# A planner-ordered backbone kernel: the output products of a recurrence step are issued inside the next step, and the planner may hold TensorE for the chain

## The chip, the cores and the metric

One core of a Trainium2 chip runs the kernel. The metric is device time in microseconds (us), the median of several runs; lower is better. Engines are called by their names in the profile: PE is TensorE (PEld its weight loads), DVE is VectorE, ACT is ScalarE, POOL is GpSimd, SP is SyncE, which issues most DMAs.

## The reference, cut to what matters

Two layers, each: a modulated norm, one wide input projection, three token mixers side by side (convolution, attention, a recurrence in both directions over the tokens), a gated merge, an output projection and an MLP. The recurrence is what the change touches:

```python
def _rwkv_scan(r, w, k, v, kk, a, s0, reverse):
    def step(s, inp):
        r_t, w_t, k_t, v_t, kk_t, a_t = inp
        sa = jnp.einsum('bhij,bhj->bhi', s, -kk_t)
        s = (s * w_t[:, :, None, :] + sa[..., None] * (kk_t * a_t)[:, :, None, :]
             + v_t[..., None] * k_t[:, :, None, :])
        return s, jnp.einsum('bhij,bhj->bhi', s, r_t)
    s_fin, ys = lax.scan(step, s0, xs, reverse=reverse)
```

There are 8 heads of 64, 256 context and 512 latent tokens, and the two directions are added. The first layer needs the output `ys` of all tokens; the second layer only that of the latent tokens.

## The kernel before

**The recurrence in chunks.** Tokens are taken in chunks of 64, two heads (a pair) and both directions at once: 12 chunks for each of 4 pairs. A pair has two halves, a half has three pieces of two chunks. So a layer has 8 halves, 48 chunk steps. For each half `prepare` makes the decayed operands on DVE and ACT, `half_t` the masked products on PE (tile `tps`), `inverse` sends a triangular matrix through DRAM, inverts 16x16 blocks on DVE and loads the result `j` back by DMA, `half_solve` finishes the inverse on PE (tiles `wps`, `jps`, with `jt` made by DVE from `j`), and `token_major` transposes what the chain needs (`trps`, `vps`, `tvps`). Then `chain_piece` runs two chunk steps, each a row of hops between PE and the other engines:

- A: `ca<-x,ar`, the state X against this chunk's operand (PE), then `rhs` (DVE); meanwhile ACT makes the decayed state `xp`.
- B: `ca<-rhs,j` and `cb<-rhs,j`, the triangular solve (PE), then `gv` (one half on ACT, one on DVE).
- C: `ca<-gv,tok` (PE), then the next state X in two DVE additions.
- Y: the output products `psy<-tr,gv` and `psy<-ar,x` (PE), eight in a step, four in the first step of a pair. Nothing in the chain needs them. After a piece's second step ACT or DVE takes `psy` into `y`.

Before, the generator asks for PE for Y right after it has issued X, ahead of the next step's A.

**What sets the order.** The engines run in program order, and that order is written by a planner, `weave` (L282), when the program is built. Every stage is a set of generators (streams). A stream yields a time from which it can go on and the engine that it wants, and the planner keeps a clock for each engine (`spend`, L220, with a cost for each instruction). It always resumes the stream that could start first; on a near tie (EPS, 0.02 us) the one that stands first in the stage's order string. In the recurrence's stage (`phase_a`) the chain C stands first or, in the first layer, directly first ("CIEKAWLRGT"); G, the stream `products` of the big weight matrices (`mmps<-hh,wh` and its kin, with `wh`, `wl` and `hh`, `hl` the two parts of weights and activations), stands near the end and takes whatever time on PE the others leave. Products that the recurrence's stage doesn't place follow in the next stage, the attention (`attend`: `sps` scores, `ap` softmax, `atps` transposes into `aat`, then `mmps<-aat,avt`), and after it the merge.

Every matrix product of the kernel is issued by one line, L227 in `product` (L228 in the changed kernel, which has one more line above it), the transposes by L239, and DVE, ACT and POOL operations by L91, so rows are told apart by their tiles. One fp32 product shows as two MATMUL records in the trace, a main product (`mmps<-hh,wh`) as one.

Of the kernel before, what the change touches and what calls it, by code (L numbers as in the profile page):

```python
# [10 lines left out]
F32 = mybir.dt.float32  # L11
F32R = mybir.dt.float32r
I32 = mybir.dt.int32
AF = mybir.ActivationFunctionType
ALU = mybir.AluOpType
# [4 lines left out]
P = 128  # L20
# [31 lines left out]
SPARE = 1.5  # L52
EPS = 0.02
BLK = 1040
CTX = (0, NCTX)
# [64 lines left out]
class Trunk:  # L120
# [161 lines left out]
    def weave(self, order, streams, until=None):  # L282

        todo = self.todo
        todo += [[g, 0.0, "PE", None, None, k] for k, g in streams.items()]
        todo.sort(key=lambda s: order.find(s[5]) % 99)
        while todo and not (until and until()):
            best, at = None, 0.0  # L290
            for s in todo:
                held, names = self.held(s[4])
                if held is None or s[3] and not s[3]():
                    continue
                t = max(s[1], self.clock[s[2]], held)
                if best is None or t < at - EPS:
                    best, at, got, since = s, t, names, held
# [6 lines left out]
            try:  # L304
                y = next(best[0])
            except StopIteration:
                todo.remove(best)
                continue
            best[1:5] = y + (None, None)[len(y) - 2:]

    def running(self, keys):
        return any(s[5] in keys for s in self.todo)

# [881 lines left out]
    def half_solve(self, st):  # L1195
# [64 lines left out]
        self.x_t = max(self.x_t, t)  # L1260

    def chain_piece(self, pi, st, y, need_y):
        pr, S, V = self.pr, self.S, self.V
        hh, ar, pc = st["hh"], st["ar"], st["pc"]
        tr, tok, gv, j, tv = st["trs"][pi], st["toks"][pi], st["gvs"][pi], st["j"], st["tvs"][pi]
        gp = 3 * hh + pi
        self.x_t = max(self.x_t, st["tok_t"][pi])
        for q in range(2):
# [4 lines left out]
            yield self.x_t, "PE"  # L1273
            if need_y and q == 0:
                psy = self.rw.tile([P, 512], F32, tag="y", name="psy", bufs=1)[:, 0:256].rearrange("p (d c t) -> p d c t", d=2, c=2)
            ga = self.rw.tile([P, 512], F32, tag="ca", name="ca", bufs=1)
# [5 lines left out]
            else:  # L1282
                for d in range(2):
                    e = self.product(ga[gr[d], 0:128], ar[:, d, c, 0, :], X[:, d, :], start=True, stop=True,
                                     tile_position=(0, 64 * gd[d]))
                if not last:
                    xp = pr.tile([P, 2, 128], F32, tag="xp", name="xp", bufs=1)
                    for d in range(2):
                        S.activation(out=xp[:, d, :], in_=X[:, d, :], func=AF.Copy, scale=pc[:, d, c:c + 1])
                yield e, "DVE"  # L1290
                rhs = pr.tile([P, 128], F32, tag="rhs", name="rhs", bufs=1)
                t = V.tensor_tensor(out=rhs, in0=ga[:, 0:128], in1=tv[:, q, :], op=ALU.add)
                yield t, "PE"
            gps = [ga[:, 256:384], gb[:, 0:128]]
            for h in range(2):
                hc = slice(64 * h, 64 * h + 64)
                for d in range(2):
# [4 lines left out]
                    V.tensor_scalar(out=gv[gr[1], 2 + q, :], in0=gps[1][gr[1], :], scalar1=-1.0, scalar2=None, op0=ALU.mult))  # L1302
            yield t, "PE"
            if not last:
# [15 lines left out]
            if need_y:  # L1320
                yield t, "PE"
                for d in range(2):
                    for h in range(2):
                        hc = slice(64 * h, 64 * h + 64)
                        e = self.product(psy[hc, d, q, :], gv[:, 2 * d + q, hc], tr[:, q, gd[d], h, :],
                                         start=True, stop=first, tile_position=(0, 64 * h))
                        if not first:
                            e = self.product(psy[hc, d, q, :], X[:, d, hc], ar[:, d, c, 1, :],
                                             start=False, stop=True, tile_position=(0, 64 * h))
        if need_y:  # L1330
            yield e, "ACT" if gp in (0, 2, 3) else "DVE"
            t0 = [x - self.c0 for x in (128 * gp, 128 * (1 - gp) if gp < 2 else 896 - 128 * gp)]
            for d in range(2):
                src = psy[:, d].rearrange("p c t -> p (c t)")
                if d == 1:
                    src = src[:, ::-1]
                dst = y[:, t0[d]:t0[d] + 128]
                if gp in (0, 2, 3):
                    t = S.activation(out=dst, in_=src, func=AF.Copy)
                else:  # L1340
                    t = V.tensor_tensor(out=dst, in0=src, in1=dst, op=ALU.add)
            st["pp"]["y_t"] = t

# [102 lines left out]
    def chain(self, l, c0):  # L1446
        for n in range(8):
            p, hh = n // 2, n % 2
            pp = self.pairs[p]
            yield 0.0, "DVE", lambda: self.halves[n] is not None and "j_t" in self.halves[n]  # L1450
            st = self.halves[n]
            yield st["j_t"], "DVE"
            yield from self.half_solve(st)
            self.solved = n
            for pi in range(3):
# [4 lines left out]
                yield from self.chain_piece(pi, st, pp["y"], 128 * (3 * hh + pi) >= c0)  # L1460
                self.pieces[n] = pi
            if hh == 1:
# [33 lines left out]
    def inputs(self, l, full, lat):  # L1496
# [5 lines left out]
        self.ready, self.stage_t = {}, 0.0  # L1502
        self.conv_n, self.x_t = 0, 0.0
        self.n_upad = 2
        if len(lat) == 1:
# [705 lines left out]
```

## Time and profile before

| | |
|---|---|
| runs, us | 2950.61, 2959.81, 2959.90; median 2959.81 |
| profiled execution, us | 2955.57 (its span 2953.7) |
| mean granted TensorE clock | 0.98 |
| PE busy | 2802.2 us (95%) |
| DVE, ACT busy | 1964.8 us (67%), 1303.1 us (44%) |
| recurrence's stage | about 125 to 595 us (first layer), 1765 to 2262 us (second layer) |

Busy time is the union of an engine's instructions; PE's are pipelined and overlap. The view of stretches gives each engine's busy time between two moments; the timeline gives start and length of instructions in order, with the engine's idle time ahead of one in brackets and what ended it.

### The profile page before, as it was taken

The page shows a single profiled execution, that of the slowest core. Times are in us where ns is not written, and L with a number is a line of the kernel's source. Part 1 is how long each engine was busy: PE and PEld are TensorE (multiplying, and loading weights), DVE is VectorE, ACT ScalarE, POOL GpSimd, SP SyncE. Part 2 cuts the span into 40 slices and gives each one's busy share as a digit, 9 for nine tenths or more (in the row PEclk, how much of TensorE's full clock was granted, in tenths as well). Part 3 has the DMA queues.
Part 4 walks back from the last instruction along what each step waited for, and adds up shares of the span by engine and source line. Part 5 has one row for each costly group of instructions (what it writes and reads, how often), then busy time and mean ns, then how long its engine had stood idle before and what let it go on. Part 6 is the DMA issues. An engine that isn't in the chain of part 4 may idle for free.

```text
span 2953.7 us, 56336 instructions
## 1 busy us (share of the span) xinstructions
PE 2802.2 (95%) x22423; PEld 2236.2 (76%) x22423; DVE 1964.8 (67%) x4313; ACT 1303.1 (44%) x2522; POOL 106.7 (4%) x181
## 2 busy tenths in 40 slices
PE   8999999988999999999999999999999888899998
PEld 6777777777777887888888777776766656788887
DVE  6777777478996658764333569898894767644445
ACT  4556555455554224231313355555554564433333
POOL 0000001010000000000000000010000100000000
PEclk9999999999999999999999999999999999999999
DMA  5232233353227733553111222232334525422223
GB/s 207 64 80 74 60 86 93 92 160 113 85 75 271 265 125 115 175 188 110 63 65 67 96 72 84 74 84 70 82 109 145 162 89 161 139 93 97 94 96 104
DMA packets 247750, 330.96 MB, mean 112 GB/s; under 512 B 118256, under 2 KB 124032, under 8 KB 247360
## 3 DMA queue, kind: packets, MB, share of 16 engines
q1 hardware_dynamic: 242160, 311.63, 33.1%
q0 software_dynamic: 3712, 14.17, 1.9%
q8 instruction: 176, 2.88, 0.4%
q10 hardware_dynamic: 1616, 1.56, 0.2%
q14 instruction: 86, 0.70, 0.1%
HBM read 266.32 MB, written 47.60 MB: 106 GB/s over the span
## 4 chain that ended last, share of the span: by engine, by line
PE 75%; DVE 12%; ACT 4%; DMA 3%; issue 3%; SPq 0%; POOL 0%; DVEq 0%; ACTq 0%; POOLq 0%
PE mmps L227 60%; PE ca L227 3%; DVE cacc L91 2%; PE psy L227 2%; DVE wl L91 2%; PE tps L227 1%; ACT wh L91 1%; DVE ast L91 1%; PE sps L227 1%; PE tvps L227 1%; PE jps L227 1%; PE atps L239 1%; PE wps L227 1%; PE trps L239 1%; DVE jt L91 1%
## 5 line engine op out<-in xcount | busy, mean ns | idle before, releaser
L227 PE MATMUL mmps<-hh,wh 128*128 128x512 f32 (+1 forms) x2344 | 851.0, 363 | 21.9 <-DVE k L91 4.9
L227 PE MATMUL mmps<-hh,wl 128*128 128x512 f32 (+1 forms) x2344 | 848.2, 362 | 10.4 <-DVE wl L91 10.4
L227 PE MATMUL mmps<-hl,wh 128*128 128x512 f32 (+1 forms) x2344 | 847.7, 362 | 3.9 <-DVE hl L91 3.8
L91 DVE TENSOR_TENSOR wl<-wr,wh 128x512 fp32r<-128x512 f32 x596 | 412.3, 692 | 492.5 <-ACT wh L91 475.7
L91 ACT ACTIVATE wh<-wr 128x512 fp32r<-128x512 f32 x596 | 375.2, 630 | 741.2 <-PE mmps L227 681.7
L227 PEld LDWEIGHTS mmps<-hh,wh 128*128 128x128 f32 x2344 | 448.2, 191 | 92.1 <-issue 16.4
L227 PEld LDWEIGHTS mmps<-hh,wl 128*128 128x128 f32 x2344 | 447.7, 191 | 82.0 <-DVE wl L91 16.7
L227 PEld LDWEIGHTS mmps<-hl,wh 128*128 128x128 f32 x2344 | 448.5, 191 | 70.2 <-issue 7.2
L227 PE MATMUL mmps<-ffl,wh 128*128 128x512 f32 (+1 forms) x792 | 279.3, 353 | 0.0
L227 PE MATMUL mmps<-ffh,wh 128*128 128x512 f32 (+1 forms) x792 | 278.1, 351 | 0.0
L227 PE MATMUL mmps<-ffh,wl 128*128 128x512 f32 (+1 forms) x792 | 277.0, 350 | 0.0
L91 DVE SCALAR_TENSOR_TENSOR cacc<-upad,dww,cacc 128x783 f32<-128x783 f32 (+1 forms) x240 | 216.3, 901 | 4.4
L227 PEld LDWEIGHTS mmps<-ffh,wh 128*128 128x128 f32 x792 | 149.1, 188 | 22.7
L227 PEld LDWEIGHTS mmps<-ffh,wl 128*128 128x128 f32 x792 | 149.0, 188 | 21.5
L227 PEld LDWEIGHTS mmps<-ffl,wh 128*128 128x128 f32 x792 | 149.4, 189 | 20.7
L91 DVE SCALAR_TENSOR_TENSOR x<-mmps,mod,x 128x512 f32<-128x512 f32 (+1 forms) x126 | 80.1, 636 | 45.6 <-PE mmps L227 45.0
L91 POOL TENSOR_TENSOR bk<-bk,pc 128x384 f32<-128x384 f32 x64 | 59.3, 958 | 1230.0 <-PE tps L227 1230.0
L91 DVE SCALAR_TENSOR_TENSOR sq<-mmps,rl 128x512 f32<-128x512 f32 x96 | 56.9, 596 | 40.2 <-ACT rl L91 40.1
L91 ACT ACT_TABLE_LOAD x64 | 82.1, 1283 | 2.5 <-PE mmps L227 1.5
L91 DVE TENSOR_REDUCE ast<-sps 128x1 f32<-128x768 f32 (+1 forms) x80 | 67.5, 844 | 20.7 <-PE sps L227 20.7
L91 ACT ACTIVATE rl<-mmps 128x512 f32<-128x512 f32 x96 | 49.3, 515 | 67.9 <-PE mmps L227 67.9
L91 DVE TENSOR_TENSOR ffl<-sq,ffh 128x768 fp32r<-128x768 f32 (+1 forms) x64 | 52.7, 824 | 37.9 <-ACT ffh L91 37.7
(316 smaller groups left out, 4404.5 us busy)
## 6 DMA issues: line engine op xcount, KB each, us to landing
wr<-in_w_dram SPq DMA_DIRECT2D x268, 256.0 KB, 2.5
wr<-in_win_dram SPq DMA_DIRECT2D x236, 256.0 KB, 2.7
modw<-in_modw_dram SPq DMA_DIRECT2D x80, 512.0 KB, 4.5
wr<-in_pw_dram SPq DMA_DIRECT2D x48, 256.0 KB, 3.0
wr<-in_wo_dram SPq DMA_DIRECT2D x44, 256.0 KB, 2.6
g<-stage SPq DMA_DIRECT2D x24, 384.0 KB, 3.5
gate<-g SPq DMA_DIRECT2D x24, 384.0 KB, 3.7
scb<-in_modw_dram SPq DMA_DIRECT2D x16, 512.0 KB, 5.7
```

The source lines that it names most:

```text
L91: f(**kw)
L227: self.nc.tensor.matmul(out, lhsT, rhs, **kw)
L239: self.nc.tensor.transpose(out, src, self.ident)
```

## The change

The step's Y products are no longer issued by the step itself. The step leaves a job (`y_job`), and `y_products` issues it in the next step right behind A, before the generator yields for `rhs`. The evictions of `psy` (`y_outs`) come after that next step's `gv`. At a half's last piece the job is done at once. The mark `pieces`, by which other streams learn that a piece is through, is set in `y_outs`, so for the first two pieces of a half one step later than before.

And a stream may now yield a fifth value, a margin. With it the planner compares streams by max(ready, clock + margin, lock) - margin in place of max(ready, clock, lock): a stream that will be ready within STICK = 0.2 us of the engine's clock counts as ready now. The chain yields it ahead of B and ahead of C, not ahead of A.

```diff
+STICK = 0.2
@@ weave
-        todo += [[g, 0.0, "PE", None, None, k] for k, g in streams.items()]
+        todo += [[g, 0.0, "PE", None, None, 0.0, k] for k, g in streams.items()]
-                t = max(s[1], self.clock[s[2]], held)
+                t = max(s[1], self.clock[s[2]] + s[5], held) - s[5]
-            best[1:5] = y + (None, None)[len(y) - 2:]
+            best[1:6] = y + (None, None, 0.0)[len(y) - 2:]
@@
+    def y_products(self):
+        if self.y_job is None:
+            return
+        st, pi, q, X, first, y = self.y_job
+        self.y_job = None
...
+        if q == 0:
+            self.psy = self.rw.tile([P, 512], F32, tag="y", name="psy", bufs=1)[:, 0:256].rearrange("p (d c t) -> p d c t", d=2, c=2)
+        for d in range(2):
+            g = 1 - (q ^ d)
+            for h in range(2):
+                hc = slice(64 * h, 64 * h + 64)
+                e = self.product(self.psy[hc, d, q, :], gv[:, 2 * d + q, hc], tr[:, q, g, h, :],
+                                 start=True, stop=first, tile_position=(0, 64 * h))
+                if not first:
+                    e = self.product(self.psy[hc, d, q, :], X[:, d, hc], ar[:, d, c, 1, :],
+                                     start=False, stop=True, tile_position=(0, 64 * h))
+        if q == 1:
+            self.y_out = (st, pi, y, e)
+
+    def y_outs(self):
...
+        yield e, "ACT" if gp in (0, 2, 3) else "DVE"
...
+            if gp in (0, 2, 3):
+                t = S.activation(out=dst, in_=src, func=AF.Copy)
+            else:
+                t = V.tensor_tensor(out=dst, in0=src, in1=dst, op=ALU.add)
+        st["pp"]["y_t"] = t
+        self.pieces[st["n_half"]] = pi
@@ chain_piece
                 for d in range(2):
                     e = self.product(ga[gr[d], 0:128], ar[:, d, c, 0, :], X[:, d, :], start=True, stop=True,
                                      tile_position=(0, 64 * gd[d]))
+                self.y_products()
...
                 t = V.tensor_tensor(out=rhs, in0=ga[:, 0:128], in1=tv[:, q, :], op=ALU.add)
-                yield t, "PE"
+                yield t, "PE", None, None, STICK
...
             t = max(S.activation(out=gv[gr[0], q, :], in_=gps[0][gr[0], :], func=AF.Copy, scale=-1.0),
                     V.tensor_scalar(out=gv[gr[1], 2 + q, :], in0=gps[1][gr[1], :], scalar1=-1.0, scalar2=None, op0=ALU.mult))
-            yield t, "PE"
+            yield from self.y_outs()
+            yield t, "PE", None, None, STICK
...
             if need_y:
-                yield t, "PE"
...
+                self.y_job = (st, pi, q, X, first, y)
+        if not need_y:
+            self.pieces[st["n_half"]] = pi
+        elif pi == 2:
+            yield t, "PE"
+            self.y_products()
+            yield from self.y_outs()
@@ chain
-                self.pieces[n] = pi
```

No instruction of PE, POOL or SP is added or dropped; a few evictions and scalings in the attention change between ACT and DVE, by a rule that looks at the planner's clocks.

**TensorE, first layer, the first chunk step with outputs and the start of the second.** Before:

```order
L227 MATMUL ca<-gv,tok 64x64 x4
L227 MATMUL mmps<-hl_188,wh 128x256
L227 MATMUL mmps<-hh_187,wl 128x256
L227 MATMUL psy<-tr,gv 64x64 x4
L227 MATMUL mmps<-hh_189,wh 128x256
L227 MATMUL mmps<-hl_190,wh 128x256
L227 MATMUL ca<-x_702,ar 64x128 x2
L227 MATMUL mmps<-hh_189,wl 128x256
L227 MATMUL mmps<-hh_191,wh 128x256
L227 MATMUL mmps<-hl_192,wh 128x256
L227 MATMUL mmps<-hh_191,wl 128x256
L227 MATMUL mmps<-hh_177,wh 128x512
```

The same place in the changed kernel:

```order
L228 MATMUL mmps<-hh_191,wh 128x256
L228 MATMUL mmps<-hl_192,wh 128x256
L228 MATMUL ca<-x_702,ar 64x128 x2
L228 MATMUL psy<-tr,gv 64x64 x4
L228 MATMUL mmps<-hh_191,wl 128x256
L228 MATMUL ca<-rhs,j 64x64
L228 MATMUL cb<-rhs,j 64x64
```

`psy` moved from between main products to right behind A (`ca<-x,ar`), and between A and B (`ca<-rhs,j`) one main product is left of five.

**TensorE, second layer, the end of the attention** (`atps` transposes the softmax rows `ap`, `mmps<-aat,avt` is the last head's value product). Before:

```order
L239 MATMUL atps<-ident,ap_26725 128x128 x3
L227 MATMUL sps<-ako,aqo 128x512
L227 MATMUL sps<-akm,aqo 128x512
L227 MATMUL sps<-ako,aqo 128x256
L227 MATMUL sps<-akm,aqo 128x256
L239 MATMUL atps<-ident,ap_26725 128x128 x3
L239 MATMUL atps<-ident,ap_26769 128x128 x6
L239 MATMUL atps<-ident,ap_26804 128x128 x6
L227 MATMUL mmps<-aat,avt 128x512 x6
L227 MATMUL mmps<-ash,onesr 128x512
```

In the changed kernel, from the last head's third row of transposes on:

```order
L240 MATMUL atps<-ident,ap_26693 128x128 x3
L228 MATMUL mmps<-hh_17315,wl 128x512
L228 MATMUL mmps<-hh_17317,wh 128x512
L228 MATMUL mmps<-hl_17318,wh 128x512
L228 MATMUL mmps<-hh_17317,wl 128x512
L240 MATMUL atps<-ident,ap_26758 128x128 x3
L228 MATMUL mmps<-hh_17319,wh 128x512
L228 MATMUL mmps<-hl_17320,wh 128x512
L228 MATMUL mmps<-hh_17319,wl 128x512
L240 MATMUL atps<-ident,ap_26758 128x128 x3
```

Main products that stood in the recurrence's stage before now stand between the attention's last transposes, where none stood.

## Rows read from the trace of the kernel before

**Rows 1.** The page: busy us (share of the span) and instructions of each engine.

```profile
PE 2802.2 (95%) x22423; PEld 2236.2 (76%) x22423; DVE 1964.8 (67%) x4313; ACT 1303.1 (44%) x2522; POOL 106.7 (4%) x181
```

**Rows 2.** Stretches: us from:to, length, busy us by engine, PEclk, DMA share, GB/s.

```profile
125.00:595.00 470.00, 460.08 (x6246) 353.62 (x6245) 333.41 (x983) 261.18 (x575) 26.23 (x43) 1.00 0.29 80
1765.00:2262.00 497.00, 478.77 (x5935) 349.82 (x5935) 414.98 (x1105) 262.96 (x570) 32.64 (x45) 1.00 0.31 86
2262.00:2440.00 178.00, 150.19 (x623) 105.69 (x622) 114.28 (x211) 105.33 (x190) 18.56 (x36) 0.94 0.46 138
870.00:1000.00 130.00, 124.56 (x1081) 103.53 (x1081) 86.61 (x124) 53.32 (x86) 0.00 (x0) 0.97 0.73 260
1300.00:1400.00 100.00, 100.00 (x573) 87.61 (x572) 51.03 (x84) 23.13 (x38) 0.32 (x1) 1.00 0.40 132
```

**Rows 3.** The tile `psy`: records, ns min/median/max, first and last start.

```profile
L227 PE MATMUL psy<-tr,gv x640: 222/222/271, 170.2 to 2261.4; 128*64 128x64 f32 x160
```

**Rows 4.** Timeline of PE, first layer, 169 to 176 us: start, us, what.

```profile
169.97 0.28 PE L227 MATMUL mmps<-hh,wl 128*128 128x256 f32 x1
170.19 0.45 PE L227 MATMUL psy<-tr,gv 128*64 128x64 f32 x8
170.57 0.39 PE L227 MATMUL mmps<-hh,wh 128*128 128x256 f32 x1
170.79 0.28 PE L227 MATMUL mmps<-hl,wh 128*128 128x256 f32 x1
...
171.59 0.28 PE L227 MATMUL mmps<-hh,wh 128*128 128x256 f32 x1
171.71 0.27 PE L227 MATMUL mmps<-hl,wh 128*128 128x256 f32 x1
...
173.21 0.40 PE L227 MATMUL mmps<-hh,wh 128*128 128x512 f32 x1
173.44 0.40 PE L227 MATMUL mmps<-hl,wh 128*128 128x512 f32 x1
...
174.58 0.34 PE L227 MATMUL psy<-tr,gv 128*64 128x64 f32 x4
...
175.25 0.49 PE L227 MATMUL mmps<-hh,wh 128*128 128x512 f32 x1
```

**Rows 5.** Timeline of all engines, a step whose Y stood right ahead of A.

```profile
180.00 0.34 PE L227 MATMUL psy<-tr,gv 128*64 128x64 f32 x4
...
180.52 0.44 PE L227 MATMUL ca<-x,ar 128*64 128x128 f32 x4
180.89 0.39 PE L227 MATMUL mmps<-hh,wl 128*128 128x256 f32 x1
180.99 0.29 DVE L91 TENSOR_TENSOR rhs<-ca,tv 128x128 f32<-128x128 f32 x1
```

**Rows 6.** Timeline, second layer, a step in which PE waited for `rhs`.

```profile
2066.11 2.03 DVE L91 SCALAR_TENSOR_TENSOR cacc<-upad,dww,cacc 128x512 f32<-128x512 f32 x2
...
2068.17 0.29 DVE L91 TENSOR_TENSOR rhs<-ca,tv 128x128 f32<-128x128 f32 x1
...
2068.52 0.27 PE L227 MATMUL ca<-rhs,j 64*64 64x64 f32 x1 [0.35 <-DVE rhs L91]
```

**Rows 7.** Timeline of PE, second layer, the end of the attention.

```profile
2417.53 0.52 PE L239 MATMUL atps<-ident,ap 128*128 128x128 f32 x3 [2.27 <-DVE ap L91]
...
2422.30 6.86 PE L227 MATMUL mmps<-aat,avt 128*128 128x512 f32 x12
```

**Rows 8.** Stretches of the same 30 us, columns as in rows 2.

```profile
2410.00:2420.00 10.00, 5.32 (x20) 3.98 (x20) 8.13 (x16) 5.86 (x13) 0.00 (x0) 0.76 0.55 185
2420.00:2430.00 10.00, 8.46 (x18) 3.88 (x18) 0.00 (x0) 1.76 (x5) 0.00 (x0) 0.73 0.00 0
```

**Rows 9.** Waits of PE, second layer's recurrence: us in total, times, longest.

```profile
PE wps L227 <- DVE jt L91: 3.9, 5, 1.2
PE jps L227 <- DVE jt L91: 3.5, 7, 1.0
```

More of the change, by code (lines that the diff above doesn't have):

```diff
@@ L286, in weave @@
         todo = self.todo
-        todo += [[g, 0.0, "PE", None, None, k] for k, g in streams.items()]
-        todo.sort(key=lambda s: order.find(s[5]) % 99)
+        todo += [[g, 0.0, "PE", None, None, 0.0, k] for k, g in streams.items()]
+        todo.sort(key=lambda s: order.find(s[6]) % 99)
         while todo and not (until and until()):
@@ L308, in weave @@
                 continue
-            best[1:5] = y + (None, None)[len(y) - 2:]
+            best[1:6] = y + (None, None, 0.0)[len(y) - 2:]
     def running(self, keys):
-        return any(s[5] in keys for s in self.todo)
+        return any(s[6] in keys for s in self.todo)
     def norm_open(self, segs, n_sq=2):
@@ L1260, in half_solve @@
         self.x_t = max(self.x_t, t)
+    def y_products(self):
[3 more added lines that the diff above has]
+        self.y_job = None
+        n, ar, tr, gv = st["n_half"], st["ar"], st["trs"][pi], st["gvs"][pi]
+        c = 2 * pi + q
+        if q == 0:
[12 more added lines that the diff above has]
+    def y_outs(self):
+        if self.y_out is None:
+            return
+        st, pi, y, e = self.y_out
+        self.y_out = None
+        S, V = self.S, self.V
+        gp = 3 * st["hh"] + pi
+        psy = self.psy
+        yield e, "ACT" if gp in (0, 2, 3) else "DVE"
+        t0 = [x - self.c0 for x in (128 * gp, 128 * (1 - gp) if gp < 2 else 896 - 128 * gp)]
+        for d in range(2):
+            src = psy[:, d].rearrange("p c t -> p (c t)")
+            if d == 1:
+                src = src[:, ::-1]
+            dst = y[:, t0[d]:t0[d] + 128]
+            if gp in (0, 2, 3):
[4 more added lines that the diff above has]
+        self.pieces[st["n_half"]] = pi
     def chain_piece(self, pi, st, y, need_y):
@@ L1264, in chain_piece @@
         hh, ar, pc = st["hh"], st["ar"], st["pc"]
-        tr, tok, gv, j, tv = st["trs"][pi], st["toks"][pi], st["gvs"][pi], st["j"], st["tvs"][pi]
+        tok, gv, j, tv = st["toks"][pi], st["gvs"][pi], st["j"], st["tvs"][pi]
         gp = 3 * hh + pi
@@ L1273, in chain_piece @@
             yield self.x_t, "PE"
-            if need_y and q == 0:
-                psy = self.rw.tile([P, 512], F32, tag="y", name="psy", bufs=1)[:, 0:256].rearrange("p (d c t) -> p d c t", d=2, c=2)
             ga = self.rw.tile([P, 512], F32, tag="ca", name="ca", bufs=1)
@@ L1320, in chain_piece @@
             if need_y:
-                yield t, "PE"
[L1322 to L1342, printed above, removed]
+                self.y_job = (st, pi, q, X, first, y)
[5 more added lines that the diff above has]
+            yield from self.y_outs()
     def pair_bonus(self, l, p):
@@ L1451, in chain @@
             st = self.halves[n]
+            st["n_half"] = n
             yield st["j_t"], "DVE"
@@ L1503, in inputs @@
         self.conv_n, self.x_t = 0, 0.0
+        self.y_job = self.y_out = None
         self.n_upad = 2
```

## The prediction, made before the changed kernel ran

> **What bounds the kernel now.** I read the page first: PE is busy 95% of the span [rows 1]. A share over the whole program doesn't say what a recurrence step costs, so I read the stretches next, and in them the two recurrence stages: PE is busy 460.1 of 470 us and 478.8 of 497 us, at the full granted clock of 1.00 [rows 2]. So it stands idle for 9.9 and 18.2 us there, and the first answer is that PE sets the pace and the chain of small hops hides behind main products. The attention of the second layer is another matter: 178 us with PE busy for 150.2, so 27.8 us idle, at a mean clock of 0.94 [rows 2].
>
> But "busy" hides something, and the timeline shows what. Main products of 256 columns in a row start 0.12 us apart (171.59, 171.71), those of 512 columns 0.23 us apart (173.21, 173.44). From a main product to Y it is 0.22 (169.97 to 170.19), and from the first main product behind Y to the second again 0.22 (170.57 to 170.79) [rows 4]. PE counts as busy through all of it. So each time the row of main products is interrupted, PE pays a price that no idle column shows, and the change takes interruptions away.
>
> The Trainium skill ("Perfetto Trace Analysis", Identifying the Most-Contended Engine) says that matmul busy share is a poor measure of what PE has left, and to look at weight loads instead. The rows agree: PEld is busy 75% and 70% of the two recurrence stages and 88% of a stretch with nothing but main products [rows 2]. Judged by the busy share alone, the change could win no more than the 28 us of idle time and would have no gain from fewer interruptions; its sum would then be terms 2 to 4 below, 2952.6.
>
> **Term 1, interruptions.** The tile view has 640 records of `psy<-tr,gv`, eight in a step, so 80 steps have a Y [rows 3]. Counted over the whole order, the main products of the recurrence's stages stand in 231 and 229 rows before and in 193 and 203 after; elsewhere there are 7 more rows. So 64 interruptions go and 7 come: 57 fewer. One costs, by what is above, 0.10 us into Y, 0.10 us for the second main product behind it, and at Y's end: sixteen Y records took 0.67 us up to a main product (174.58 to 175.25) [rows 4] and 0.52 up to A (180.00 to 180.52) [rows 5], another 0.15. That is 0.35. The trace of before has no A with Y behind it. If that joint costs nothing, as the one from Y to A, 0.35 is right; if it costs like A to a main product, only the first two parts are won, 0.20. I take 0.30, nearer to the row of Y to A, where tile sizes are the same: 57 x 0.30 = **17.1 us less** (11.4 to 20).
>
> **Term 2, TensorE held idle.** The order now has 41 steps (27 and 14) where only Y stands between A and B. The earliest B behind A: A lasts 0.44, `rhs` starts 0.03 later and lasts 0.29 [rows 5], and B follows its end by 0.06 (2068.46 to 2068.52) [rows 6], together 0.82. A takes PE for 0.37 at most (180.52 to 180.89) and Y for 0.52 [rows 5], together 0.89. So with DVE free Y just covers the wait, and I give these steps 0.1 each for the joint that isn't known, 4 us. With DVE not free it is different: two `cacc` operations of 2.03 us stood ahead of one `rhs`, and PE waited 0.35 although six main products had filled the time [rows 6]. There are 88 steps with both a B and a C behind a wait (96 less the 8 first ones), so 176 places at which the planner may now hold PE. For lateness that its clocks don't know I add 6 us, an estimate: one place in four, 0.14 each. Together **10 us more** (0 to 44, the latter with 0.25 at every place). What is queued behind such a wait on PE are main products, and nobody waits for these soon.
>
> **Term 3, main products that move.** In the second layer's stage the order has 62 main products of 512 columns fewer (14.3 us at 0.23), and 53 of them reappear inside the attention, between the last transposes above all, where PE had gaps such as 2.27 us [rows 7]. They are 12.2 us of work for 27.8 us of idle time [rows 2]. The stage ends earlier by their time, and the attention starts earlier. It gets longer where four products (0.9 us) stand in a shorter gap and by three more interruptions; I take 3 us for that: **9 us less** (0 to 12). In the first layer 87 main products leave the stage (about half of each size, 15 us), but the attention there doesn't take them up (977 main products where 986 stood); they come behind it, where PE is busy 124.6 of 130 us [rows 2]. They are moved, not hidden: nothing, at best the 5 us that stand idle there.
>
> **Term 4, the clock at the end of that attention.** The granted clock is 0.76 and 0.73 of full in the last stretches, after gaps on PE [rows 8], between the levels 1.2 and 2.4 GHz, and the twelve records of the last value product take 6.86 us, 0.57 each [rows 7] where 0.23 is usual [rows 4]. With main products in the gaps I expect the full level: 12 x 0.34 = **4 us less** (0 to 6).
>
> **At no cost, with the cover.** The two evictions of `psy` move behind `gv`, on the same engines; there they run while PE does C and the state waits for C, and before they ran beside the next A. If C came at once, the state update would wait for 2 x 0.29 us on DVE in half of the pieces. `pieces` is set a step later for two pieces of three; the streams that read it prepare the next half, six steps ahead. No DMA is added, and SP and POOL pass nothing.
>
> **The sum.** 2955.6 - 17.1 + 10 - 9 - 4 = 2935.5, against the profiled execution's own time. That lies 4.2 us below the median of the runs and among them, so I leave it there: **2936 us**, 0.8% under the median. About 0.3%, 9 us, is what a measurement of this kernel can tell from no change.
>
> **Rivals.** *One, slower: the held PE costs more than it brings.* DVE is busy 415 of 497 us in the second stage [rows 2], and whatever it runs ahead of `rhs`, `gv` or X now meets a PE with less filling. Price: 0.25 us at each of 176 places, 44 us in place of 10, so 2970. It decides from about 0.17 us a place, where the 20 us are gone. For it speaks the 0.35 us under cover [rows 6]; against it, that PE idles in the whole second stage only for 18.2 us with the same DVE work.
>
> *Two, no change: the inverse sets the length of the stage, not the steps.* Each half waits for `j` by DMA before `half_solve`, and PE's longest waits in that stage are `wps` and `jps` for `jt`, 7.4 us [rows 9]. If `j` doesn't land earlier, the steps only reach it sooner; the 15 us of the first layer are then paid afterwards and the 9 us of term 3 stay away: 2936 + 15 + 9 = 2960. Against it: the preparation of a half also waits for an earlier half's chain, so `j` does come earlier.
>
> *Three, slower: the clock falls in the recurrence.* It stayed at 1.00 with 28 us of short idle times [rows 2]. At 0.97, as behind the first attention [rows 2], 967 us of stages would take 3% more, 29 us: 2965 or above. The Trainium skill ("TensorE: Matmul & The Clock Gate", A second HAM failure mode) describes a PE that idles briefly and often between groups of matmuls and swings between both levels, which would do this here; the rows of before don't show it.
>
> *Four: the planner doesn't do as told.* The order rules this out for Y; only the hold could be empty, and then terms 1 and 2 shrink together: about 2945.
>
> **How the numbers follow.** Forecast 0.67, rival one 0.09, two 0.13, three 0.03, four 0.08. The forecast's own span is 2918 (20 us, 5 us idle, 12 us, 5 us in the first layer, 6 us for the clock) to 2950 (11 us won, 20 us idle, half of terms 3 and 4). For 8 in 10 it reaches up to rival two: 2914 to 2960. Faster by over 0.3% (below 2951): the forecast nearly whole and most of four, 0.73. Within 0.3%: rival two and the forecast's upper end, 0.16. Slower: 0.11.
>
> **What would show it.** Right: behind A the trace has Y with no main product between, then B within 0.1 us of `rhs`' end; steps shorter; PE idle in the two stages up by about 10 us together while the stages shrink by 15 to 22 us each; the second attention with half of its idle time and the clock near 1.00 at its end. Wrong: PE waits for `rhs` or `gv` of over 0.2 us in most steps (rival one), stages as long as before with longer waits for `jt` (two), a clock below 1.00 in the stages (three).

## The result, and the profile after

| | before | after |
|---|---|---|
| median, us | 2955.69 (4 runs, 2950.61 to 2959.90) | 2914.53 (4 runs, 2913.63 to 2917.97) |
| ratio, 95% interval | | 0.9863 [0.9847, 0.9879] |
| profiled execution, us (span) | 2955.57 (2953.7) | 2913.63 (2911.8) |
| mean granted TensorE clock | 0.980 | 0.986 |

The changed kernel is faster by 41 us, 1.4%. The forecast was 2936 us, a gain of 20 us, so the direction was right and the size half of what came; the time lies at the very bottom of the range. A second measurement of the same kernel, in the last group of experiments, gave 0.9868 [0.9844, 0.9893].

The page's line of busy times (columns as in [rows 1]), after:

```profile
PE 2768.5 (95%) x22423; PEld 2229.7 (77%) x22423; DVE 1961.5 (67%) x4311; ACT 1299.9 (45%) x2522; POOL 104.9 (4%) x181
```

PE executes as many instructions as before and is busy for 33.7 us less (2802.2 in [rows 1]). So four fifths of the gain lie inside the time that counts as busy, where the forecast looked for its term 1, and in the granted clock.

The stretches tell where. The next fences show before, then after: from the first chain product of a layer to its merge, then (for each layer) the recurrence, from the first chain product to the last, and the attention behind it, up to its last transposes. Columns as in [rows 2].

```profile
167.70:1109.00 941.30, 898.67 (x8678) 715.00 (x8677) 681.78 (x1505) 462.92 (x941) 40.90 (x72) 0.98 0.39 122
1818.30:2558.60 740.30, 683.12 (x6437) 500.67 (x6435) 562.91 (x1324) 383.79 (x782) 45.66 (x72) 0.97 0.38 111
167.70:583.40 415.70, 406.40 (x5616) 309.54 (x5615) 290.42 (x863) 228.59 (x513) 22.09 (x36) 1.00 0.28 77
583.40:855.10 271.70, 247.18 (x1328) 201.41 (x1324) 231.08 (x400) 147.83 (x290) 18.81 (x36) 0.96 0.37 115
1818.30:2261.50 443.20, 427.15 (x5356) 311.19 (x5354) 366.73 (x979) 231.43 (x512) 27.10 (x36) 1.00 0.31 85
2261.50:2422.10 160.60, 135.92 (x595) 97.76 (x592) 111.03 (x205) 96.79 (x178) 18.56 (x36) 0.96 0.51 154
```

```profile
167.00:1084.40 917.40, 879.01 (x8677) 710.09 (x8677) 680.88 (x1505) 460.27 (x939) 41.44 (x72) 0.99 0.40 125
1793.50:2516.70 723.20, 670.83 (x6436) 500.93 (x6435) 560.98 (x1322) 383.39 (x784) 43.34 (x72) 0.98 0.39 113
167.00:559.80 392.80, 380.33 (x5528) 298.14 (x5528) 287.61 (x859) 221.03 (x504) 22.53 (x36) 1.00 0.29 77
559.80:821.40 261.60, 241.85 (x1318) 196.42 (x1314) 230.72 (x401) 148.14 (x289) 18.91 (x36) 0.97 0.38 118
1793.50:2213.00 419.50, 405.00 (x5292) 301.29 (x5292) 362.24 (x974) 226.99 (x505) 24.80 (x36) 1.00 0.30 83
2213.00:2380.10 167.10, 146.83 (x648) 107.99 (x646) 113.02 (x207) 99.64 (x185) 18.55 (x36) 0.96 0.51 150
```

The first layer is shorter by 23.9 us, the second by 17.1; the rest of the program keeps its length within about 1 us. The clock stays at 1.00 in both recurrences. The recurrences are shorter by 22.9 and 23.7 us, but not all of that is won: they hold 88 and 64 PE records fewer (x5616 to x5528, x5356 to x5292), main products that are now done elsewhere. What the forecast did not have is the fourth row: the first layer's attention, for which it put down nothing, is 10.1 us shorter with ten PE records fewer, and those ten are worth only some 2 us.

A step of the kind that the change is for, first layer, timeline of PE and DVE (start, us, what; compare [rows 5]):

```profile
183.08 0.44 PE L228 MATMUL ca<-x,ar 128*64 128x128 f32 x4
183.25 0.25 PEld L228 LDWEIGHTS psy<-tr,gv 128*64 128x64 f32 x3
183.36 0.34 PE L228 MATMUL psy<-tr,gv 128*64 128x64 f32 x4
...
183.56 0.29 DVE L92 TENSOR_TENSOR rhs<-ca,tv 128x128 f32<-128x128 f32 x1 [0.62 <-PE ca L228]
183.59 0.34 PE L228 MATMUL psy<-tr,gv 128*64 128x64 f32 x4
...
183.71 0.34 PE L228 MATMUL psy<-ar,x 128*64 128x64 f32 x4
...
183.97 0.27 PE L228 MATMUL ca<-rhs,j 64*64 64x64 f32 x1
```

A at 183.08, Y from 183.36, `rhs` done at 183.85, B at 183.97 and no bracket ahead of it: PE never stood still. A to B takes 0.89 us. The trace has 41 steps with Y alone between A and B, the number that the order promised, and in 33 of them PE has no idle time ahead of B.

### The profile page after: what moved, and what is told of

Same layout as the page of the kernel before. It is cut to its first block, busy times and chain, and to the rows that moved or that the text cites. A ratio compares the mean times of both kernels' runs of the same rounds, so it can differ in the third digit from the quotient of the medians.

```text
span 2911.8 us, 56372 instructions
## 1 busy us (share of the span) xinstructions
PE 2768.5 (95%) x22423; PEld 2229.7 (77%) x22423; DVE 1961.5 (67%) x4311; ACT 1299.9 (45%) x2522; POOL 104.9 (4%) x181
## 4 chain that ended last, share of the span: by engine, by line
PE 73%; DVE 14%; ACT 4%; DMA 3%; issue 2%; SPq 0%; DVEq 0%; POOL 0%; ACTq 0%; POOLq 0%
PE mmps L228 60%; PE ca L228 3%; DVE cacc L92 2%; DVE wl L92 2%; DVE ast L92 2%; PE tps L228 1%; ACT wh L92 1%; PE psy L228 1%; PE jps L228 1%; PE wps L228 1%; PE tvps L228 1%; DVE ap L92 1%; DVE x L92 1%; PE atps L240 1%; PE sps L228 1%
## 5 line engine op out<-in xcount | busy, mean ns | idle before, releaser
L92 ACT ACTIVATE stage<-mmps 128x512 f32<-128x512 f32 (+1 forms) x116 | 59.1, 510 | 51.7 <-PE mmps L228 48.7
```

Of the source, the lines that this page charges most:

```text
L92: f(**kw)
```

## The experiments

Two theories ran through them. *S*: the 41 us are made in the steps (fewer interruptions) and follow from the edit. *P*: the edit is worth about half of that; the other half is that every edit makes the planner write another order (a plan) for everything around the steps, and this plan happens to have fewer long waits and less time at half clock.

For all of them I kept one account, for each layer from its first chain product to its merge (the first two stretches above): PE's idle time; the time in which the records show the granted clock at 1.2 in place of 2.4 GHz ("half clock"); and the interruptions, which is how often PE goes from a main product to something else, counted over the records in order of start. Sums of both layers:

| kernel | ratio to before, 95% | both layers, us | idle | half clock | interruptions |
|---|---|---|---|---|---|
| before | 1 | 1681 | 99.8 | 71.6 | 622 |
| after | 0.9863 [0.9847, 0.9879] | 1641 | 90.8 | 44.4 | 565 |
| e1 deferral alone | 0.9985 [0.9972, 0.9998] | 1672 | 101.2 | 88.7 | 574 |
| e2 hold alone | 0.9962 [0.9949, 0.9976] | 1665 | 92.1 | 58.0 | 613 |
| e3 before, EPS 0.03 | 0.9977 [0.9964, 0.9990] | 1667 | 95.3 | 58.0 | 614 |
| e4 before, EPS 0 | 1.0013 [1.0001, 1.0026] | 1684 | 99.1 | 92.2 | 612 |
| e5 after, EPS 0.03 | 0.9913 [0.9892, 0.9933] | 1653 | 94.9 | 58.1 | 561 |
| e6 after, EPS 0 | 0.9918 [0.9903, 0.9932] | 1654 | 95.4 | 64.9 | 561 |
| e7 after, hold 0.4 | 0.9905 [0.9887, 0.9923] | 1657 | 101.6 | 51.2 | 543 |
| e8 after, hold at A too | 0.9921 [0.9897, 0.9944] | 1657 | 97.1 | 64.9 | 549 |
| e9 after, again | 0.9868 [0.9844, 0.9893] | 1647 | 93.9 | 47.8 | 565 |
| e10 change in layer 1 | 0.9926 [0.9906, 0.9946] | 1665 | 94.8 | 68.3 | 588 |
| e11 change in layer 2 | 0.9933 [0.9911, 0.9955] | 1661 | 94.1 | 58.1 | 599 |
| e12 after, hold 0.1 | 0.9908 [0.9888, 0.9928] | 1658 | 98.0 | 64.9 | 552 |

Ratios are of medians, the other columns of one profiled execution each. A least-squares line through the 28 layer stretches of these 14 executions, with one constant for each layer, gives length = constant + **1.20** (+-0.12) x idle + **0.32** (+-0.05) x half-clock time + **0.28** (+-0.02) x interruptions (one standard error each), and misses no stretch by more than 3.0 us. It is a correlation; but the price of an interruption lies in the range that the joints of the trace gave beforehand (0.20 to 0.35), and the price of the clock has a second, rougher witness: the 27 runs of before in the first group lie between 0.978 and 0.985 in mean clock and get 1.5 us shorter for each 0.001, which is 5.9 us of half clock, so 0.25 us for one (the 7 and 11 runs of before in the later groups give 0.2 and 0.4).

**e1 and e2: the two halves of the change alone.** e1 is the changed kernel without the hold, e2 the kernel before with the hold ahead of B and C and Y where it was.

```diff
e1: -STICK = 0.2
    +STICK = 0.0
e2: the kernel before, and in chain_piece, ahead of B and ahead of C:
    -yield t, "PE"
    +yield t, "PE", None, None, STICK
    (and the margin in the planner, as in the change)
```

> The change without the hold: STICK = 0, so Y is issued behind the next A, but TensorE is never held. Counted in its order, main products stand in 198 and 212 rows in the two recurrence stages (before 231 and 229, the change 193 and 203), and 20 main products move into the second attention (the change: 53). Theory S (the gain is made in the steps: fewer interruptions, shorter steps): 45 interruptions fewer at 0.35 us are 16 us, moved products 4 us, so about 2936, half of the change's gain. Theory P (half of the change's gain was made outside the steps, because any new plan shifts where TensorE waits and falls to half clock in the first attention and merge): the stages give the same 16 us, but the time may lie anywhere between 2920 and 2950, and the difference from 2936 is found between the end of the first recurrence stage and 1150 us.

> The change without the deferral: Y stays ahead of the next A, but the planner holds TensorE by 0.2 us for B and C. Rows of main products 227 and 222 (11 fewer than before), 39 main products move into the second attention. Theory S: 4 us for interruptions, 9 us for moved products, less some 5 us of added idle time, so about 2948. Theory P: 2930 to 2965, again with the difference in the first attention and merge.

The deferral alone takes away 48 of the 57 interruptions, 13 us by the account, and yet the kernel gains only 4 us: PE idles no less, and there are 17 us more at half clock. The hold alone takes away 9 and gains 11 us, by 8 us less idle time and 14 us less half clock; S had 2948 for it and P 2930 to 2965, so the 2942 that came lies nearer to S and doesn't decide. The deferral doesn't have its gain where its edit works. That speaks for P, but each is also a new plan, so alone they can't be told from chance; hence the next four. One other reading of e1 stays open: that the deferral pays only together with a hold. No second plan with the deferral alone was run.

**e3 and e4: the kernel before, with other plans.** Nothing but the near tie of the planner is changed, so the steps are those of before.

```diff
e3: -EPS = 0.02
    +EPS = 0.03
e4: -EPS = 0.02
    +EPS = 0.0
```

> The kernel before with one number of the planner moved: EPS 0.03 in place of 0.02, which says when two streams are a tie. Neither part of the change is in it; the order shifts all the same (rows of main products 225 and 230, nearly as before). Theory S: within 5 us of before, 2951 to 2961. Theory P: more than 8 us away from before, up or down, with the difference in idle and half-clock time of TensorE outside the recurrence.

> The kernel before with EPS 0 (rows of main products 223 and 232, and 113 main products fewer inside the first attention). Theory S: within 5 us of before. Theory P: more than 8 us away, up or down.

With the steps as before, the time moves by -7 and +4 us (intervals 3 to 11 us less, and 0 to 8 us more), and the interruptions by 8 and 10. Neither theory had these sizes: S allowed 5 us, P asked for more than 8. A plan by itself is worth several microseconds either way, in step with idle and half-clock time, which is a weaker P.

**e5 and e6: the change, with the same other plans.**

```diff
e5, e6: the changed kernel with the edits of e3 and of e4
```

> The change with the planner's slack EPS at 0.03 in place of 0.02: same steps, another plan for all that lies around them. Theory S (the gain is made in the steps and follows from the edits): 2914 again, within 5 us, with the half-clock time near 74 us. Theory P (about half of the 41 us is the particular plan: long waits and half-clock time in the first layer's attention and merge that the plan before had and this one has not): 2922 to 2935, half-clock time 90 to 110 us, and the stages as short as in the change (about 393 and 420 us, corrected by main products moved).

> The change with EPS 0: a third plan. The kernel before lost 4 us with EPS 0 (2959 against 2954). Theory S: 2914 to 2920. Theory P: 2922 to 2940, the difference to the change outside the two recurrence stages and in step with the half-clock time (34 us of it were worth about 17 us between the kernel before and the change).

Both lie where P put them, at 2931 and 2934 us: the change keeps its 53 or 54 interruptions less and loses some 15 us of its gain. Set against before with the same EPS, the change is worth 0.9913/0.9977 = 0.9936 and 0.9918/1.0013 = 0.9905, so 19 and 28 us, and 40 with the EPS that was shipped, each uncertain by 5 to 7 us. In the profiles the pair with 0.03 is the cleanest: idle (95.3 and 94.9) and half clock (58.0 and 58.1) are equal in sum, 53 interruptions fall away, and both layers together get shorter by 13.7 us, 0.26 for each. That is one execution of each kernel, and a layer varies by some 5 us from one to the next (below), so 0.26 is a rough figure. The two layers in e3, then in e5, stretches as above:

```profile
171.40:1096.80 925.40, 889.57 (x8680) 709.03 (x8680) 679.28 (x1504) 456.87 (x939) 41.33 (x72) 0.99 0.40 124
1806.00:2547.30 741.30, 681.80 (x6435) 501.13 (x6435) 561.26 (x1322) 384.15 (x784) 44.45 (x72) 0.97 0.38 110
```

```profile
170.30:1089.50 919.20, 882.14 (x8680) 712.97 (x8679) 681.72 (x1506) 464.62 (x943) 41.95 (x72) 0.99 0.40 125
1798.70:2532.50 733.80, 676.03 (x6436) 503.28 (x6435) 560.67 (x1322) 383.45 (x783) 42.45 (x72) 0.97 0.38 112
```

The first layer of e5 is as short as the changed kernel's; it is the second that lacks 11 us, with 5.4 us more idle and 10 us more at half clock.

**e7, e8 and e12: the dose of the hold.** The hold at 0.4 and at 0.1 in place of 0.2, and 0.2 ahead of A too.

```diff
e7:  -STICK = 0.2          e12: -STICK = 0.2
     +STICK = 0.4               +STICK = 0.1
e8:  -            yield self.x_t, "PE"
     +            yield self.x_t, "PE", None, None, STICK
```

> The change with the hold STICK at 0.4 in place of 0.2: TensorE is held longer for B and C. The order has 374 rows of main products in the two stages in place of 396. If interruptions cost 0.3 us and holding costs next to nothing (what the change's trace shows): 22 x 0.3 = 7 us less, 2908, if the idle time in the stages grows by less than 3 us. If the hold's price appears with the dose: idle time in the stages up by 10 us or more from 27 us, and 2918 or above. Theory P adds some 10 us to either side by the other plan, outside the stages.

> The change with the same hold of 0.2 ahead of A too. The order has 379 rows of main products in the stages in place of 396: 17 x 0.3 = 5 us less, and 2909, if A's hold costs as little as B's and C's. If X comes late by more than the hold, as it may with two operations behind each other on DVE: idle time in the stages up by 5 us or more, 2915 to 2920. Theory P adds some 10 us to either side, outside the stages.

> The change with the hold at 0.1 in place of 0.2, a fifth plan with the deferral: 386 rows of main products in the stages where the change has 396. By the account of the runs so far (length of a layer = a constant + 1.17 x idle + 0.30 x half-clock time + 0.28 x interruptions) the interruptions alone give 3 us less than the change. If the plan sets idle and half-clock time as by chance: 2922 to 2935 like the four siblings. If the small hold is simply right and large ones hurt: 2910 to 2918.

All three have fewer interruptions than the changed kernel, 13 to 22, and are slower than it, by 12 to 17 us if the ratios are laid on 2956 us. For e8 that is more than any branch of its expectation allowed; for e12 it is the branch of a chance plan, at its upper end. With 0.4 the price of holding shows: PE's waits ahead of `ca` for `rhs` in the second recurrence (us in total, times, longest), first in the changed kernel, then in e7:

```profile
PE ca L228 <- DVE rhs L92: 2.1, 6, 0.6
```

```profile
PE ca L228 <- DVE rhs L92: 4.8, 14, 0.7
```

Summed over both layers and both waits, small gaps included, PE stands 0.4 us ahead of B and C before, 7.1 us in the changed kernel and 15.1 us with 0.4. The 22 interruptions that 0.4 saves, 6 us, are worth less than the 8 us that it adds. With 0.1 the waits at B and C come to 4.2 us, and with the hold at A too those at A, B and C to 10.5 (8.4 in the changed kernel): little either way, and yet both kernels are no better than e5 and e6. The five siblings of the changed kernel, five plans with the deferral and a hold, lie within 0.9905 and 0.9921. Since e5 and e6 hold by 0.2 as well, a dose of 0.2 is not special; the plan that came with it is.

**e9: the changed kernel again, beside e10 to e12.** Were the first four runs a chance of the executions?

> The changed kernel itself, unaltered, beside the kernels of this group. Its four siblings with other plans took 2931 to 2934 us (0.991 to 0.992 of before). If its particular plan is what makes it faster than these: 0.986 of before again, 2914 to 2918, half-clock time 70 to 85 us. If its first times were a chance of the executions: 0.990 to 0.992, 2922 to 2932, and half-clock time of 95 to 115 us as in the siblings.

0.9868 beside 0.9863: the plan's advantage holds in other executions of the same order too. Only the ratio says so. The time itself, 2922 us, is where a chance of the executions had been put, but before was slower in this group too (2959 us); and the half-clock time of the whole profile is 93 us, above the 70 to 85 that were expected. In the profile the clock is not the same as in the first one: 27.3 us of half clock in the first layer where the first execution had 13.7, 20.5 in the second where it had 30.7.

**e10 and e11: the change in one layer.** The generator asks which layer it is in; the other layer has PE's order of before, main products and all.

```diff
+        late = self.c0 == 0        # e10: first layer;  e11: self.c0 != 0
...
                 self.y_job = (st, pi, q, X, first, y)
+                if not late:
+                    yield t, "PE"
+                    self.y_products()
...
+        elif not late:
+            yield from self.y_outs()
...
-            yield t, "PE", None, None, STICK
+            yield t, "PE", None, None, STICK if late else 0.0
```

> The change in the first layer alone: there TensorE's order is the change's, instruction by instruction, in the second layer the order of before. If each layer's gain belongs to its own order: the first layer's stretch shorter by 24 us as in the change (10 of them in the steps, 0.3 x 34 interruptions), the second layer's as before: 0.992, 2931 to 2933. If what differs outside the steps is chance of the executions: 0.995 or above, 2941 and more.

> The change in the second layer alone, the first layer in the order of before. If each layer's gain belongs to its own order: 17 us less, 0.994, 2939 to 2941, 7 of them by 23 interruptions fewer, the rest by idle and half-clock time. If the second layer gains only by its interruptions: 0.997 to 0.998, 2948 to 2950.

0.9926 x 0.9933 = 0.986: the layers add up to the whole, and each layer's gain belongs to its own order. They also give a second and a third execution of each order. The two layers in e10, then in e11:

```profile
167.60:1087.50 919.90, 882.30 (x8677) 712.67 (x8677) 681.06 (x1505) 460.48 (x939) 41.44 (x72) 0.99 0.40 124
1796.70:2541.10 744.40, 687.19 (x6435) 503.89 (x6434) 563.24 (x1324) 384.07 (x781) 45.62 (x72) 0.97 0.37 110
```

```profile
173.10:1107.40 934.30, 891.90 (x8677) 708.90 (x8677) 681.94 (x1505) 462.92 (x941) 40.99 (x72) 0.99 0.39 123
1816.60:2543.20 726.60, 674.93 (x6436) 502.38 (x6435) 559.86 (x1322) 383.27 (x784) 44.05 (x72) 0.97 0.39 113
```

Over these executions the first layer takes 941.3 and 934.3 us in the old order and 917.4, 926.7 (e9) and 919.9 in the new one: 16.4 us less on average. The second takes 740.3 and 744.4, and 723.2, 720.0 (e9) and 726.6: 19.1 us less. A single execution of a layer varies by some 5 us, which is why the means, and not the one pair of profiles, are used below.

**What a plan changes, in one place.** The longest wait of the first layer in the old order is not in the recurrence but in the attention behind it. Timeline of before, PE and DVE, 683 to 692 us:

```profile
683.23 0.40 PE L227 MATMUL mmps<-hl,wh 128*128 128x512 f32 x1
...
687.29 0.68 DVE L91 TENSOR_TENSOR aqk<-aqk,rope 128x512 f32<-128x512 f32 x1
688.30 0.69 DVE L91 TENSOR_TENSOR asw<-asw,rope 128x512 f32<-128x512 f32 x1 [0.32 <-DMA asw<-k]
689.02 0.69 DVE L91 TENSOR_TENSOR aqk<-aqk,asw 128x512 f32<-128x512 f32 x1
689.63 1.28 DVE L91 TENSOR_TENSOR wl<-wr,wh 128x512 fp32r<-128x512 f32 x2
...
690.37 0.80 PE L227 MATMUL mmps<-hh,wl 128*128 128x512 f32 x1 [6.74 <-DVE wl L91]
690.97 0.63 PE L227 MATMUL mmps<-hh,wh 128*128 128x512 f32 x1
691.39 0.63 PE L227 MATMUL mmps<-hl,wh 128*128 128x512 f32 x1
```

A main product needs `wl`, the low part of its weights, and DVE makes that behind a row of the attention's operations, one of which waits for a DMA (0.32). PE stands for 6.74 us, and then its main products start 0.42 us apart where 0.23 is usual [rows 4]: the granted clock is 0.50 there, the level of 1.2 GHz.

```profile
690.00:692.00 2.00, 1.63 (x4) 1.34 (x5) 2.00 (x4) 0.59 (x1) 1.02 (x2) 0.50 0.15 55
```

The kernel e11, the other execution of this order, has the same wait (6.81). No other plan has one as long: the longest wait behind the recurrence of the first layer is 3.2 us in the three executions of the new order, and between 3.0 and 5.2 in the nine others. The waits of PE in the first layer's attention, old order, then new:

```profile
PE mmps L227 <- DVE wl L91: 6.9, 2, 6.7
PE sps L227 <- ACT ap L91: 3.7, 2, 3.3
PE atps L239 <- DVE ast L91: 2.8, 2, 2.3
```

```profile
PE sps L228 <- ACT ap L92: 5.9, 4, 3.2
PE mmps L228 <- ACT stage L92: 3.9, 6, 3.0
PE mmps L228 <- DVE wl L92: 3.5, 3, 2.3
```

Other waits have come in place of the long one; in all, PE's idle time in this attention falls by 4.2 us, from 24.5 to 20.3 on average. The change has no edit there. The attention starts with other main products left over and the planner's clocks stand elsewhere, so all ties fall anew.

## Why the forecast was right in direction and half in size

The steps of its sum, beside what the means over executions of the same order show. For the length of a stretch that is two executions of the old order and three of the new.

| step | forecast, us | shown, us |
|---|---|---|
| 1: 57 interruptions fewer | -17.1 | -16.0 |
| 2: PE idle in the recurrences | +10 | +2.6 |
| 3: main products into the second attention | -9 | -9.7 |
| 3: first layer's attention and merge, beyond the products moved | 0 | -12.4 |
| 4: clock at the end of the second attention | -4 | 0 |
| sum | -20.1 | -35.5 |

The lengths of the two layers give -35.5 as well; the lines of the table overlap by an us or two here and there, which cancels. The medians give 41 us in the first group and, by the ratio, 39 in the last; what these few profiles leave of that, 4 to 6 us, is assigned to no step.

**Term 1 was right**, in count and price. The trace has 57 interruptions fewer, as the order told, and one costs 0.28 by the account and 0.26 in the pair e3, e5, where 0.30 was taken. The joint that the trace of before didn't show, A with Y behind it, costs nothing that can be seen: A to Y 0.28 and A to B 0.89 in the step above. The Trainium skill ("TensorEngine Tiling (Array Packing)", Key Properties) says that a change of tiling mode drains TensorE; it gives no price, and here a main product is the full array and the chain's products are parts of it. The runs agree that there is a price, 0.28 us for going there and back; that it is the draining that costs it, no run here shows. The view that counts matmul busy time, by which fewer interruptions win nothing, is refuted: the gain is mostly in busy time.

**Term 2 was mis-sized.** At B and C themselves it was nearly right: 7.1 us of new waits where 10 were put down, and Y covers `rhs` in 33 of 41 steps. But the sum added them to the idle time of before as if that stayed. It didn't: PE's idle time grows by 3.8 us in the first recurrence (8.8 to 12.6) and falls by 1.2 in the second (15.6 to 14.4), 2.6 in all, so other waits there fell by 4 us. The waits that rival two feared are among them, in the second recurrence (compare [rows 9]):

```profile
PE wps L228 <- DVE jt L92: 2.5, 4, 1.0
...
PE jps L228 <- DVE jt L92: 1.9, 5, 0.7
```

4.4 us where 7.4 stood, and 5.3 in e9. Rival two is refuted by this and by the length of the stages.

**Term 3, second layer: right**, if one takes the mean. 62 main products left the recurrence (14.3 us), and the attention grew by 4.6 us on average (6.5 in the first pair) where 3 had been put down, because a part of the products found an idle gap: PE's idle time there falls by 4.7 us, from 24.9 to 20.2 on average, where the prediction's sign had half of it gone. This is a matter of the plan too: of the five siblings, e7 and e8 move as many there (390 main products in the attention, 387 in the changed kernel, 334 before), the other three hardly any (335 to 353).

**Term 3, first layer: the step that failed.** "They are moved, not hidden: nothing" holds for the 87 products: the stretch behind the attention, up to the first modulation product (`nearps`), grows by 16.8 us, and they are paid in full. But with that sentence the attention and the rest of the merge behind `nearps` were put at nothing too, without a reason. They became shorter by 7.2 and 5.2 us, the attention from 270.6 to 263.4 us on average: the 6.74 us wait is gone and, in two of three executions, two waits for the DMA of the scores' operands (2.1 and 2.2 us) shrink to 0.5 us or less. Some 2 of the 7.2 us are the ten main products that left the attention. This gain needs no edit of the steps: e3, which has the steps of before, has a first layer of 925.4 us where the old order has 937.8 on average, with only 6 interruptions fewer. So the old order seems to have been an unlucky draw there; that is one execution of e3. The rows that would have raised the question were in the trace: a wait of 6.74 us with a stretch at half clock behind it, in a stage whose order was known to change. What could not be had from them is the sign. Five other plans with the deferral and a hold show what the gain is without this plan: both layers 24.5 us shorter than the old order on average, 19 of it interruptions, and 0.9905 to 0.9921 in time, 23 to 28 us. The forecast of 20 fits those; the shipped plan has some 13 us on top.

**Term 4 was misread.** The end of the second attention, PE and then the stretches (compare [rows 7, 8]):

```profile
2378.76 0.52 PE L240 MATMUL atps<-ident,ap 128*128 128x128 f32 x3 [0.80 <-DVE ap L92]
...
2381.17 5.31 PE L228 MATMUL mmps<-aat,avt 128*128 128x512 f32 x12
```

```profile
2368.00:2378.00 10.00, 8.64 (x44) 6.45 (x43) 7.86 (x17) 9.94 (x19) 0.00 (x0) 1.00 0.24 79
2378.00:2388.00 10.00, 8.88 (x30) 4.94 (x30) 1.81 (x3) 2.83 (x6) 0.00 (x0) 1.00 0.19 54
```

The gaps are filled as foreseen, the clock is 1.00 there, and the value product takes 5.31 us where it took 6.86. But 5.31 us is simply its length at the full clock. The trace of before had it, for an earlier head of the same attention, with a clock of 1.00 around it:

```profile
2315.96 5.31 PE L227 MATMUL mmps<-aat,avt 128*128 128x512 f32 x12
```

In both traces the records of 512 columns of this product start 0.43 us apart at 1.00, in every head. The 0.23 that the term took as usual is the distance of main products, another kind of product; 1.5 us were to be won in place of 4, and they were won. The stretch from the last transposes to the merge is as long as before all the same, 136.7 us against 136.3 on average: it now holds nine main products more (501 where 492 stood), some 2 us, the nine of the 62 that the attention didn't take. So the table has 0.

**The clock.** Rival three foresaw a clock that falls in the recurrence; in the changed kernel it stays at 1.00 in both. Between the two orders half-clock time falls by 17 us on average, which the account prices at 5.4 us; it is contained in the steps above. Account and lengths agree but for 4 us: interruptions -16.0, idle time 8.4 us less x 1.20 = -10.1, clock -5.4, sum -31.5 of -35.5.

**What stays open** is why this one plan idles less than its siblings in the second layer (52.2 us where they have 55.7 on average, 30.7 at half clock where they have 40.3). No single wait explains it, and with five siblings it may be no more than the best of six draws.

## What to carry to other kernels

Where a planner writes the order, an edit in one stage is also a new draw for all other stages: give the forecast a term for that, sized by building the kernel before with one or two harmless other plans, and judge an edit over several plans, not over one pair. The price of an interruption can be read from start-to-start distances at the joints, though PE counts as busy through all of it. Work that nobody waits for can fill a short wait of the chain; here it had the chain's tile sizes and about the length of the wait, and no other filling was tried.

## What the runs showed of the hardware that was not expected

**Behind a wait of a little over a microsecond the clock fell in some places, and in others it did not.** e1, first recurrence, the wait and the stretches around it:

```profile
204.30 0.68 PE L228 MATMUL tvps<-gv,ta 64*64 64x64 f32 x16 [1.11 <-DVE j L92]
```

```profile
200.00:206.60 6.60, 5.13 (x177) 4.05 (x177) 2.35 (x6) 2.31 (x6) 0.00 (x0) 1.00 0.12 42
206.60:213.40 6.80, 6.80 (x75) 4.74 (x72) 2.69 (x7) 1.27 (x4) 0.00 (x0) 0.50 0.01 2
213.40:220.00 6.60, 6.60 (x90) 5.60 (x90) 5.05 (x14) 1.66 (x4) 1.96 (x3) 1.00 0.00 0
```

PE idles for 1.47 of 6.6 us, and the stretch after that, in which it never idles, runs at 0.50, the level of 1.2 GHz. e2 has the same behind a wait of 1.54 us for `jt` that ends at 260.6 us: the mean clock from 260 to 272 us is 0.57. But such a wait alone doesn't decide it. The changed kernel's first profile, with 12.5 us of short idle times in the same recurrence and waits of 1.42 and 1.33 us among them, has no half clock in it, nor has before, with waits of 1.55 and 1.33 us. The longer wait of the changed kernel, and the stretch around it:

```profile
364.53 0.36 PE L228 MATMUL mmps<-hh,wh 128*128 128x256 f32 x1 [1.42 <-DVE r L92]
```

```profile
358.00:372.00 14.00, 12.04 (x244) 9.43 (x242) 13.02 (x25) 6.87 (x12) 0.00 (x0) 1.00 0.65 174
```

The Trainium skill ("TensorE: Matmul & The Clock Gate", A second HAM failure mode) tells of a PE that idles briefly between groups of products and swings between both levels; the stretches of e1 and e2 agree with it, the two recurrences without half clock do not.

**The same order does not fall to half clock at the same places.** Of the three executions of the new order in the first layer, the recurrence has 0, 6.8 and 3.4 us at half clock, with idle times of 12.5, 12.3 and 13.0 us. So the clock's part of a difference between two profiles is partly chance, and only the mean clock of several runs (0.9855 for the changed kernel in its first runs, 0.981 for before in the first group) tells a difference of kernels.
